# Scaling softmax weights: one VectorE multiplication with repeated inverse sums in place of two VectorE and two ScalarE operations

## The chip, the cores and the metric

The kernel runs on one core of a Trainium2 chip. The metric is the device time of one execution in microseconds (us); the median of the runs is used. The core's engines are named as in the profile: PE (TensorE, matmuls and transposes), DVE (VectorE), ACT (ScalarE), POOL (GpSimd) and SP (SyncE). POOL and SP mostly issue DMAs here. Each engine works through its own queue in order and waits at its head for semaphores of the others.

## What is computed

One layer of a streaming encoder: 1024 tokens, width 1024, float32. The part that the change touches is the attention with a window of three 64-token chunks, 16 query heads and 2 key/value heads of 64 dimensions, and a learned sink for each head:

```python
s = einsum('bnqhgd,bnkhd->bhgnqk', qc, kb) * HEAD_DIM ** -0.5
s = where(valid, s, -1e30)
m = maximum(max(s, axis=-1), sink)
p = exp(s - m)
denom = sum(p, axis=-1) + exp(sink - m)
o = einsum('bhgnqk,bnkhd->bnqhgd', p / denom, vb)
```

Before it stands one RMSNorm and a large input projection (queries, keys, values, gates and the inputs of the second branch); after it the gates, two output projections, the residual and a last RMSNorm. The change concerns `p / denom`.

## The kernel before, in words

**The matmul frame.** Most of the time goes into projections. They are done two output tiles at a time by `gemm_pair` (a "pair"), as seven products of 512 x 512 quarters with pre-added operands, named by their right-hand forms `b11`, `t1`, `t2`, `b21`, `t3`, `b22`, `t4`, in this order. Each product is 12 matmuls of 128x512 (line L362): operands are split in a rounded high part and a low remainder, and high x high, high x low and low x high are added up. The weight halves `wh` (a cast on ACT, L176) and `wl` (a subtraction on DVE, L177) are made by `split_next` while products run; there are three buffers of each, so a cast waits until the product that read the buffer's old content is through. After some products ACT copies and DVE adds the accumulator (L380, L384, L387, L392, L397, L401).

**Attention rides in the hooks.** From about 305 us to 585 us the eleven pairs that project gates call a hook after each product, and the hook advances a generator, `attention()`. It goes through 32 steps: 2 key/value groups x 8 query tiles of 128 tokens x 2 parities. Counting from 0, step n is a `softmax_stage` in two halves (chunk c = 0, 1, each 64 queries of 4 heads laid out as two sets of 128 rows, i = 0, 1), the `weight_stage` of step n - 2 (transposes of the weights) and the `value_stage` of step n - 3 (weights times values). About three steps fall in one pair.

**One softmax step.** For each chunk PE makes two score tiles `ps_sc` (L1442), ACT copies them to `sl` (L1448), DVE adds their two halves, negates and takes the row bound into `nmax` (L1454, a custom instruction with a second one that reads its accumulator), and ACT exponentiates in place and sums the rows into `sums` (L1470, again with a read of the accumulator). The chunk's exponentials are issued behind the copies of the next chunk. After the second chunk `rest_of_step` adds the sink's share (L1484 on DVE, L1485 on ACT, L1486 on DVE), takes reciprocals `inv` (L1488) and scales the weights: chunk 0 by two `tensor_scalar_mul` on DVE (L1493), chunk 1 by two multiplications on ACT (L1495). The weights of a step lie in one tile `pr` of 128 x 2 x 384; chunk 1 has the first 192 columns and chunk 0 the last 192 (in the first query tile of a group, 128 and 64).

**What reads them.** In `weight_stage` PE transposes six blocks of `pr` (L1515, four in the first tile): first the two blocks that lie in chunk 0's columns, then the two in chunk 1's, then the two in the middle that hold both. ACT and DVE then split the transposed weights (`pT`, `pTb`), and PE multiplies them by the values (L1550, L1555). ACT copies and DVE adds the result into `aT` (L1563, L1564).

**Order.** The order of each engine's queue is made by the framework's scheduler from the program, its dependencies and `after` (an order without a wait). A change of one instruction can therefore move others.

Of the kernel before, what the change touches and what calls it, by code (L numbers as in the profile page):

```python
# [26 lines left out]
AF = mybir.ActivationFunctionType  # L27
# [3 lines left out]
P = 128  # L31
# [21 lines left out]
def hybrid_tile(  # L53
# [16 lines left out]
    nc = tc.nc  # L70
# [12 lines left out]
    def bank(tag, dt=F32):  # L83
        return psum.tile([P, 512], dt, name=nm("ps_" + tag), tag="ps_" + tag, bufs=2)

    def mtile(shape, dt, tag, bufs, pool=None):
        return (pool or main).tile(shape, dt, name=nm(tag), tag=tag, bufs=bufs)
# [11 lines left out]
    def after(second, first):  # L99

        tc.add_manual_dep(
            second.ins,
            first.ins.name,
            mybir.DependencyInfo(mybir.DependencyClass.NoSync, mybir.DependencyReason.DATA),
            reason="order",
        )
# [521 lines left out]
    def scale_of(t):  # L628
        xt = x_in[t] if t in x_in else load_x(t)
        ss = mtile([P, 1], F32, "st1", 16)  # L630
        if t < 1:
            base = mtile([P, 1], F32, "st1", 16)
            square = nc.scalar.activation(junk[:, 0:HALF], xt[:, 0:HALF], AF.Square, accum_out=ss[:])
            z = xt[:, HALF:D]
            by_vector = nc.vector.tensor_tensor_reduce(
                junk[:, HALF:D], z, z, 4.0 / D, 4.0 * EPS, op0=ALU.mult, op1=ALU.add, accum_out=base[:]
            )
            after(by_vector, g_low)
            squares.append(square)
            return xt, rstd_of(ss[:], 1.0 / D, base[:])  # L640
        square = nc.scalar.activation(junk[:], xt[:], AF.Square, accum_out=ss[:])
        squares.append(square)
        if t == 7:
            after(square, casts[11])
        elif t > 2:

            after(square, casts[2 * t - 3])
        return xt, rstd_of(ss[:], 1.0 / D)
# [197 lines left out]
    first = scale_of(0)  # L846
# [259 lines left out]
    bias = []  # L1106
# [310 lines left out]
    def small():  # L1417
        return mtile([P, 2, 2], F32, "sm", 12, aheads)

    def window_of(t, c):  # L1420

        return (64 * c, 64 * c + 192) if t else (P, P + 64 * (c + 1))

    def softmax_stage(g, t, par, qt):

        kt = keys[g, t][0]
        q_of = qt[:].rearrange("p i (q c) -> p c (i q)", c=2)
        nmax, sums = small(), small()  # L1430
        n_pr[0] += 1
        pr = mtile([P, 2, 384], F32, f"pr{n_pr[0] % 2}", 1, weights_pool)
        held_in = {}
        sinks_of = (v[:, 4 * g + par : 4 * g + par + 3 : 2] for v in (sink_sb, nsink_sb))
        sk, nsk = sinks_of
        for c in range(2):
            lo, hi = window_of(t, c)
            wide = hi - lo
            scores, halves, copies = [], [], []
            for i in range(2):  # L1440
                sc = bank("sc")[:, 0 : 2 * wide].rearrange("p (f k) -> p f k", f=2)
                nc.tensor.matmul(  # L1442
                    sc, q_of[:, c, i * P : (i + 1) * P], kt[:, :, lo:hi], start=True, stop=True
                )
                scores.append(sc)
            for i, sc in enumerate(scores):
                two = mtile([P, 2, 192], F32, "sl", 2, aheads)[:, :, 0:wide]
                copies.append(nc.scalar.copy(two, sc))  # L1448
                halves.append(two)
            for i, two in enumerate(halves):  # L1450
                at = 192 * (1 - c) if t else P * (1 - c)
                held_in[c, i] = v = pr[:, i, at : at + wide]
                bounds.append(
                    nc.vector.tensor_tensor_reduce(  # L1454
                        v,
                        two[:, 0, :],
                        two[:, 1, :],
                        1.0,
                        nsk[:, i : i + 1],
                        op0=ALU.add,  # L1460
                        op1=ALU.min,
                        accum_out=nmax[:, c, i : i + 1],
                    )
                )
            finish_chunk(copies[-1])

            def rest_of_chunk(copied, c=c):
                for i in range(2):
                    v = held_in[c, i]
                    e = nc.scalar.activation(  # L1470
                        v, v, AF.Exp, bias=nmax[:, c, i : i + 1], scale=-1.0, accum_out=sums[:, c, i : i + 1]
                    )
                    if copied is not None:
                        after(e, copied)
                if c == 1:
                    rest_of_step()

            unfinished.append(rest_of_chunk)
            if c == 0:
                yield  # L1480

        def rest_of_step():
            es = small()
            nc.vector.tensor_add(es[:], sk.unsqueeze(1).broadcast_to([P, 2, 2]), nmax[:])  # L1484
            nc.scalar.activation(es[:], es[:], AF.Exp)  # L1485
            nc.vector.tensor_add(es[:], es[:], sums[:])  # L1486
            inv = small()
            nc.vector.reciprocal(inv[:], es[:])  # L1488
            for c in range(2):
                for i in range(2):  # L1490
                    v = held_in[c, i]
                    if c == 0:
                        nc.vector.tensor_scalar_mul(v, v, inv[:, c, i : i + 1])  # L1493
                    else:
                        nc.scalar.mul(v, v, inv[:, c, i : i + 1])  # L1495
            held.append(pr)

        yield
# [3 lines left out]
    def finish_chunk(copied=None):  # L1502

        if unfinished:
            unfinished.pop(0)(copied)
# [66 lines left out]
    def attention():  # L1572
# [14 lines left out]
        for n, step in enumerate(steps):  # L1587
            if n >= 2:
                weigh(n - 2)
                yield  # L1590
            halves = softmax_stage(*step, qT.pop(0))
            next(halves)
            yield
            next(halves)
            if n + 2 < len(steps):
                qT.append(query_stage(*steps[n + 2]))
            if n in (0, 2):
                value_loads(*tiles[n // 2])
            yield
            if n >= 3:  # L1600
                value(n - 3)
                yield
# [427 lines left out]
    for p in range(4):  # L2030
        n, t, acc, x11 = N_PAIRS + p, T_ORDER[p], accs[p], firsts[p]
# [92 lines left out]
        wide = HALF // 2  # L2124
# [98 lines left out]
```

## Time and profile before

| | |
|---|---|
| median of 3 runs | 894.31 us (894.05 to 894.41) |
| profiled execution | 894.7 us, its span 892.9 us |
| granted PE clock, mean | 0.998 |
| busy over the span | PE 99%, PE weight loads 82%, DVE 77%, ACT 65%, POOL 17% |
| chain that ended last | PE 92%, ACT 3%, DVE 2% |

The span is the time from the first to the last instruction of the program; the execution's own time is 1.8 us longer. A busy PE is not one at its peak: matmuls overlap their successors, and a record of 0.39 us can be followed by the next after 0.23 us. To see what PE loses at a place, compare start times, not busy shares. In listings by time, the columns are the start, the duration, the engine, the line, the operation, what it writes and reads, and how many instructions were merged; in square brackets the idle time before it and what ended it.

### The profile page before, as it was taken

The numbers are of one execution on the slowest core, as the hardware profiler recorded it, in microseconds if no ns is written. First come the engines' busy times: TensorE is split into PE (matmuls) and PEld (weight loads), VectorE is DVE, ScalarE is ACT, GpSimd is POOL, SyncE is SP. The second block draws the span as 40 slices with busy tenths as digits, with TensorE's granted clock in tenths as the row PEclk, the third lists the DMA queues.
The fourth block names the chain that finished last, engine by engine and source line by source line (L and its number), as shares of the span: only waits on it lengthen the run. The fifth ranks groups of instructions, "written<-read, shape, count | busy, mean of one in ns | idle before, by whom it ended". The sixth has DMA issues, their size and how long they took to land.

```text
span 892.9 us, 13164 instructions
## 1 busy us (share of the span) xinstructions
PE 881.7 (99%) x4117; PEld 731.4 (82%) x4117; DVE 684.9 (77%) x1362; ACT 580.1 (65%) x1189; POOL 150.9 (17%) x217
## 2 busy tenths in 40 slices
PE   8999999999999999999999999999999999999996
PEld 6888888888888888888888888888888888888885
DVE  7979966566686778888878888847796578579886
ACT  6875533334445489989989899955685385467443
POOL 3322222203030001111211011101121121110012
PEclk9999999999999999999999999999999999999999
DMA  9998888958778667888786789989899789998533
GB/s 332 211 268 222 268 206 172 176 153 265 250 252 286 214 189 189 210 185 195 179 236 210 237 225 222 250 290 383 308 289 376 276 231 258 298 307 282 179 119 118
DMA packets 131410, 212.40 MB, mean 238 GB/s; under 512 B 12778, under 2 KB 59882, under 8 KB 131340
## 3 DMA queue, kind: packets, MB, share of 16 engines
q1 hardware_dynamic: 108808, 148.62, 50.0%
q0 software_dynamic: 22384, 62.67, 31.6%
q8 instruction: 33, 0.54, 0.2%
q14 instruction: 37, 0.30, 0.1%
q10 hardware_dynamic: 148, 0.27, 0.1%
HBM read 146.37 MB, written 86.11 MB: 260 GB/s over the span
## 4 chain that ended last, share of the span: by engine, by line
PE 92%; ACT 3%; DVE 2%; issue 1%; DMA 1%; POOL 0%; SPq 0%; ACTq 0%; DVEq 0%
PE ps_mm L362 42%; PE ps_o L362 24%; PE ps_tp L362 7%; PE ps_sc L362 3%; PE ps_tp L793 2%; PE ps_o L793 2%; PE ps_mm L793 2%; PE ps_tp L1515 2%; PE ps_sc L1442 2%; PE ps_tp L1112 2%; PE ps_o L1550 1%; PE ps_sc L793 1%; ACT wh L176 1%; DVE wl L177 1%; PE ps_o L1555 1%
## 5 line engine op out<-in xcount | busy, mean ns | idle before, releaser
L176 ACT CAST wh<-s 128x1024 fp32r<-128x1024 f32 (+1 forms) x79 | 79.4, 1006 | 75.2 <-PE ps_mm L362 23.5
L177 DVE TENSOR_TENSOR wl<-wr,wh 128x512 fp32r<-128x512 f32 (+1 forms) x77 | 72.0, 937 | 58.0 <-ACT wh L176 57.9
L177 DVE TENSOR_TENSOR wl<-s,wh 128x1024 fp32r<-128x1024 f32 (+1 forms) x79 | 92.9, 1176 | 11.8 <-ACT wh L176 11.7
L176 ACT CAST wh<-wr 128x512 fp32r<-128x512 f32 (+1 forms) x77 | 63.0, 819 | 55.9 <-PE ps_mm L362 31.5
L1448 ACT COPY sl<-ps_sc 128x384 f32<-128x384 f32 (+2 forms) x128 | 51.8, 456 | 9.9 <-DVE sm L1454 9.9
L362 PE MATMUL ps_o<-T_t1h,wh 128*128 128x512 f32 x148 | 57.9, 391 | 0.0
L362 PE MATMUL ps_o<-T_t1h,wl 128*128 128x512 f32 x148 | 57.7, 390 | 0.0
L362 PE MATMUL ps_o<-T_t1l,wh 128*128 128x512 f32 x148 | 57.6, 389 | 0.0
L1470 ACT ACTIVATE pr<-pr,sm 128x192 f32<-128x192 f32 (+2 forms) x128 | 56.2, 444 | 0.1
L1454 DVE CUSTOM_DVE_ANT_0 pr<-sl,nsink_sb 128x192 f32<-128x192 f32 (+2 forms) x128 | 48.0, 399 | 9.9 <-ACT sl L1448 8.8
L362 PE MATMUL ps_mm<-T_b11h,wh 128*128 128x512 f32 x140 | 54.9, 392 | 0.0
L362 PE MATMUL ps_mm<-T_t3h,wh 128*128 128x512 f32 x140 | 54.7, 390 | 0.0
L362 PE MATMUL ps_mm<-T_b11l,wh 128*128 128x512 f32 x140 | 54.6, 390 | 0.0
L362 PE MATMUL ps_mm<-T_t2h,wh 128*128 128x512 f32 x140 | 54.6, 390 | 0.0
L362 PE MATMUL ps_mm<-T_b11h,wl 128*128 128x512 f32 x140 | 54.6, 390 | 0.0
L362 PE MATMUL ps_mm<-T_t3h,wl 128*128 128x512 f32 x140 | 54.6, 390 | 0.0
L362 PE MATMUL ps_mm<-T_t2l,wh 128*128 128x512 f32 x140 | 54.6, 390 | 0.0
L362 PE MATMUL ps_mm<-T_t3l,wh 128*128 128x512 f32 x140 | 54.5, 390 | 0.0
L362 PE MATMUL ps_mm<-T_t2h,wl 128*128 128x512 f32 x140 | 54.5, 389 | 0.0
L362 PE MATMUL ps_mm<-T_t4h,wh 128*128 128x512 f32 x136 | 53.2, 391 | 0.3 <-DVE x L397 0.3
L362 PE MATMUL ps_mm<-T_t4h,wl 128*128 128x512 f32 x136 | 53.0, 390 | 0.0
L362 PE MATMUL ps_mm<-T_t4l,wh 128*128 128x512 f32 x136 | 52.9, 389 | 0.0
(432 smaller groups left out, 2448.5 us busy)
## 6 DMA issues: line engine op xcount, KB each, us to landing
wr<-in_w_dram SPq DMA_DIRECT2D x86, 256.0 KB
sums<-in_w_dram POOLq DMA_DIRECT2D x20, 512.0 KB, 7.0
s<-sums SPq DMA_DIRECT2D x20, 512.0 KB
q_hl<-qhl SPq DMA_DIRECT2D x16, 512.0 KB
q<-q_hl SPq DMA_DIRECT2D x64, 128.0 KB
y_dr<-x POOLq DMA_DIRECT2D x28, 256.0 KB, 6.8
g<-in_w_dram POOLq DMA_DIRECT2D x12, 512.0 KB, 6.8
wr<-in_w_dram SPq DMA_DIRECT2D x11, 512.0 KB
```

The source lines that it names most:

```text
L176: hi_of.append(nc.scalar.copy(hi, src))
L177: lo_of.append(nc.vector.tensor_sub(lo, src, hi.bitcast(F32)))
L362: nc.tensor.matmul(acc, lt, rt, start=fresh and k == 0 and n == 0, stop=k == 3 and n == 2, skip_group_check=True,)
L793: mm = nc.tensor.matmul(acc[:], lt, rt, start=fresh and k == 0 and n == 0, stop=stops and k == 3 and n == terms[-1], skip_group_check=True,)
L1112: nc.tensor.matmul(pm[:, t * P : (t + 1) * P], xh[:, half * 4 + t, g * P : (g + 1) * P], bias[-1][1][:, g % 4, :], start=True, stop=True,)
L1442: nc.tensor.matmul(sc, q_of[:, c, i * P : (i + 1) * P], kt[:, :, lo:hi], start=True, stop=True)
L1448: copies.append(nc.scalar.copy(two, sc))
L1454: nc.vector.tensor_tensor_reduce(v, two[:, 0, :], two[:, 1, :], 1.0, nsk[:, i : i + 1], op0=ALU.add, op1=ALU.min, accum_out=nmax[:, c, i : ...
L1470: e = nc.scalar.activation(v, v, AF.Exp, bias=nmax[:, c, i : i + 1], scale=-1.0, accum_out=sums[:, c, i : i + 1])
L1515: nc.tensor.transpose(dst, pr[:, i, block * P : block * P + width], ident[:])
L1550: nc.tensor.matmul(po[:, first], va[1][:, vs], a[:, n, first], start=n == 0, stop=n == 1, skip_group_check=True)
L1555: nc.tensor.matmul(po[:, cs], vb[c][:, vs], b[c][:], start=t == 0, stop=True, skip_group_check=True)
```

## The change

The four scalings of a step become one `tensor_mul` on DVE over the whole tile `pr`, whose second operand is `inv` read with a step of zero along the columns (two such instructions in each of the four steps on a group's first tile, since the two chunks have different widths there). For that, `nmax`, `sums` and so `inv` are stored by place in `pr`: chunk c at index 1 - c.

```diff
-                        accum_out=nmax[:, c, i : i + 1],
+                        accum_out=nmax[:, 1 - c, i : i + 1],
...
-                        v, v, AF.Exp, bias=nmax[:, c, i : i + 1], scale=-1.0, accum_out=sums[:, c, i : i + 1]
+                        v, v, AF.Exp, bias=nmax[:, 1 - c, i : i + 1], scale=-1.0, accum_out=sums[:, 1 - c, i : i + 1]
...
-            for c in range(2):
-                for i in range(2):
-                    v = held_in[c, i]
-                    if c == 0:
-                        nc.vector.tensor_scalar_mul(v, v, inv[:, c, i : i + 1])
-                    else:
-                        nc.scalar.mul(v, v, inv[:, c, i : i + 1])
+            spans = ((0, 2, 384),) if t else ((0, 1, P), (1, 1, 64))
+            start = 0
+            for first, chunks, wide in spans:
+                v = pr[:, :, start : start + wide].rearrange("p i (c k) -> p i c k", c=chunks)
+                by = inv[:, first : first + chunks].rearrange("p c i -> p i c").unsqueeze(3)
+                nc.vector.tensor_mul(v, v, by.broadcast_to(list(v.shape)))
+                start += wide
```

The scheduler then orders some neighbours in another way. The first place is PE's queue behind the product `t3` of a pair, where the transposes of a step stand (step 12; the other pairs with such a place read alike). Before:

```order
L362 MATMUL ps_mm_4054<-T_t3h_754,wl_4034 128x512
L1515 MATMUL ps_tp_4278<-ident,pr_761_4090 128x128 x4
L1515 MATMUL ps_tp_4286<-ident,pr_761_4090 128x128 x2
L1442 MATMUL ps_sc_4298<-k_4140,q_4142 128x384
L1442 MATMUL ps_sc_4300<-k_4140,q_4142 128x384
L362 MATMUL ps_o_4113<-T_b22h_398,wh_4033 128x512
```

And now:

```order
L1442 MATMUL ps_sc_4261<-k_4106,q_4108 128x384
L1515 MATMUL ps_tp_4241<-ident,pr_761_4059 128x128 x4
L1515 MATMUL ps_tp_4249<-ident,pr_761_4059 128x128 x2
L1442 MATMUL ps_sc_4263<-k_4106,q_4108 128x384
L362 MATMUL ps_o_4079<-T_b22h_398,wh_4002 128x512
```

One of the two score matmuls now stands ahead of the transposes (at step 3 both do, and the first matmul of `b22` as well). The second place is ACT's queue half a pair earlier, from the copy behind `t1` (L384) to the cast of the weights of `t4` (L176), where the ACT scalings of step 11 stood. Before:

```order
L384 ACTIVATE x_4057<-ps_o_4113 128x512
L1495 ACTIVATE pr_727_3962<-pr_727_3962,sm_4107 128x192 x2
L1448 COPY sl_4132<-ps_sc_4128 128x384
L1448 COPY sl_4134<-ps_sc_4130 128x384
L1470 ACTIVATE pr_761_4090,sm_4089<-pr_761_4090,sm_4088 128x192 x2
L1563 COPY aT_4046<-ps_o_4145 64x2x4x64
L176 CAST wh_4171<-wr_3698 128x512
```

And now:

```order
L384 ACTIVATE x_4026<-ps_o_4079 128x512
L1448 COPY sl_4098<-ps_sc_4094 128x384
L1448 COPY sl_4100<-ps_sc_4096 128x384
L1470 ACTIVATE pr_761_4059,sm_4058<-pr_761_4059,sm_4057 128x192 x2
L1563 COPY aT_4015<-ps_o_4111 64x2x4x64
L176 CAST wh_4137<-wr_3676 128x512
```

Nothing else moved there; the two scalings are gone and all behind them stands directly behind L384. The third place is DVE's queue at the seam of the two groups (steps 15 and 16), between the row bounds of step 16 and the update L397 of an accumulator that PE's product `t4` waits for. It reads L262, L1564, L263, L264, L265, L397 before; now it reads L1564, L262, L264, L263, L397, L265, so that L397 stands behind four operations instead of five. On SP some loads changed places with neighbours (weights `wr`, keys `k`, values `vb`, stores of `x`); POOL's order is the same.

## The prediction

> **What bounds the kernel now.** I read the page first, then the busy times by stage, then what PE waits for in the attention stage, then the chain and the queues around its longest waits.
>
> ```profile
> 305.00:585.00 280.00, 277.90 (x1362) 232.06 (x1361) 230.18 (x660) 249.16 (x694) 39.15 (x50) 1.00 0.79 210
> ```
>
> The columns after the length are PE, weight loads, DVE, ACT and POOL. In the only stage that the change touches PE is busy for 277.9 of 280 us. ACT (249.2) is fuller than DVE (230.2); over the whole kernel it is the other way round. So nothing can be won but what PE loses here by waiting:
>
> ```profile
> PE ps_tp L1515 <- DVE pr L1493: 1.7, 6, 0.3
> PE ps_mm L362 <- DVE x L397: 0.3, 1, 0.3
> PEld ps_tp L1515 <- PE ps_mm L362: 5.0, 8, 0.7
> PEld ps_sc L1442 <- ACT sl L1448: 1.2, 6, 0.3
> ```
>
> The transposes of the weights (L1515) wait for exactly the scaling that is changed. The third row has eight waits, all in front of transposes (the release is put down to PE, which had long been done); they are the eight steps 3, 6, 9, 12, 21, 24, 27 and 30, whose transposes stand behind `t3`. In all other steps they stand behind `t2` or `b11`, and the listing by time has them 0.8 to 2.9 us behind the end of the scaling, the marginal step 1 apart. One of the eight, step 12:
>
> ```profile
> 417.11 0.39 PE L362 MATMUL ps_mm<-T_t3h,wl 128*128 128x512 f32 x1
> 417.20 0.80 ACT L1495 ACTIVATE pr<-pr,sm 128x192 f32<-128x192 f32 x2
> 417.34 0.54 DVE L1493 TENSOR_SCALAR pr<-pr,sm 128x192 f32<-128x192 f32 x2
> 417.80 0.90 PE L1515 MATMUL ps_tp<-ident,pr 128*128 128x128 f32 x6 [0.31 <-DVE pr L1493]
> 418.46 0.60 PE L1442 MATMUL ps_sc<-k,q 128*128 128x384 f32 x2
> 418.90 0.39 PE L362 MATMUL ps_o<-T_b22h,wh 128*128 128x512 f32 x1
> ```
>
> Matmuls of 128x512 follow each other by 0.23 us, so PE could have begun at 417.34 and began at 417.80: 0.46 us lost. What decides is therefore when the scaling starts and how long it takes. The chain tells where its start comes from (start, length, what):
>
> ```profile
> 409.82 0.57 ACT aT L1563
> ...
> 414.41 0.95 ACT wh L176
> ...
> 415.38 1.22 DVE wl L177
> ...
> 417.42 0.25 DVE pr L1493
> ...
> 417.80 0.79 PE ps_tp L1515 x5
> ```
>
> It is ACT's queue, from 409.8 to 415.4 without a pause, and then the subtraction `wl` on DVE that waits for ACT's last cast and stands ahead of the reciprocal and the scaling. ACT's queue further back:
>
> ```profile
> 406.76 0.58 ACT L384 ACTIVATE x<-ps_o 128x512 f32<-128x512 f32 x1
> 407.36 0.80 ACT L1495 ACTIVATE pr<-pr,sm 128x192 f32<-128x192 f32 x2
> 408.07 0.84 ACT L1448 COPY sl<-ps_sc 128x384 f32<-128x384 f32 x2
> 409.18 0.39 PE L362 MATMUL ps_mm<-T_t2l,wh 128*128 128x512 f32 x1
> 409.25 0.45 ACT L1470 ACTIVATE pr<-pr,sm 128x192 f32<-128x192 f32 x1
> 409.81 0.58 ACT L1563 COPY aT<-ps_o 64x512 f32<-64x512 f32 x1
> 410.42 0.62 ACT L176 CAST wh<-wr 128x512 fp32r<-128x512 f32 x1
> ```
>
> ACT is late here by its own work: the scores that L1448 copies and the sums that L1563 copies had been made 1.9 and 2.8 us before. Among that work are the two scalings of step 11, which the change removes. How far ACT can move ahead is limited by the cast at 410.42, which must wait until the `t2` product has read the buffer: its last matmul with `wh` starts at 409.18 and ends at 409.57.
>
> **The change part by part.** The durations (busy us, mean ns):
>
> ```profile
> L1493 DVE TENSOR_SCALAR pr<-pr,sm 128x192 f32<-128x192 f32 x56 | 15.3, 315 | 0.4
> L1495 ACT ACTIVATE pr<-pr,sm 128x192 f32<-128x192 f32 x56 | 22.4, 447 | 3.2 <-DVE sm L1488 3.0
> L262 DVE TENSOR_TENSOR s<-wr 128x512 f32<-128x512 f32 x23 | 15.8, 686 | 6.8 <-DMA wr<-in_w_dram 4.9 <-issue 1.8
> L177 DVE TENSOR_TENSOR wl<-s,wh 128x1024 fp32r<-128x1024 f32 x71 | 87.5, 1232 | 11.8 <-ACT wh L176 11.7
> ```
>
> *The new instruction.* No row has 128x768 with a repeated operand. Bounds are the 512 (0.686 us) and the 1024 (1.232 us) of the same operation; halfway between lies 0.96 us, and I take that, since a zero step asks for no more data. Against 0.54 us for the two it replaces, the scaling ends 0.42 us later from the same start, and DVE does 28 x 0.42 = 12 us more in the stage (230 to 242 of 280).
>
> The Trainium skill, "VectorE: DVE Perf Modes" (section "The perf-mode tier table"), speaks against the change: float32 `tensor_tensor` runs at one element a cycle, `tensor_scalar` at two. Its formula, (N + 151) / 0.96, gives an estimate of 957 ns for 768, which is what the two rows above give, so the sum by it is the same. What the rule leaves out is ACT's part.
>
> *ACT's relief.* 56 operations of 0.447 us go (22.4 us busy), and 8 more in the first tiles. On the path lies only the pair that stands ahead of the cast at 410.42: without it L1448 starts 0.8 us sooner, and so does all behind it down to the cast, which can go back from 410.42 to 409.60 at most. From there on chain and order are as before, so the scaling of step 12 would start at about 417.34 - 0.80 = 416.54. By the listing steps 21, 24 and 30 are like it (their casts start 0.8 to 0.9 us after the buffer is free). In the others the cast already stands near that limit:
>
> ```profile
> 332.10 0.39 PE L362 MATMUL ps_mm<-T_t2l,wh 128*128 128x512 f32 x1
> 332.71 0.62 ACT L176 CAST wh<-wr 128x512 fp32r<-128x512 f32 x1
> 339.76 0.54 DVE L1493 TENSOR_SCALAR pr<-pr,sm 128x192 f32<-128x192 f32 x2
> 341.56 0.39 PE L362 MATMUL ps_o<-T_b22l,wh 128*128 128x512 f32 x1
> 383.38 0.39 PE L362 MATMUL ps_mm<-T_t2l,wh 128*128 128x512 f32 x1
> 384.16 0.62 ACT L176 CAST wh<-wr 128x512 fp32r<-128x512 f32 x1
> 391.21 0.54 DVE L1493 TENSOR_SCALAR pr<-pr,sm 128x192 f32<-128x192 f32 x2
> 392.78 0.39 PE L362 MATMUL ps_o<-T_b22h,wh 128*128 128x512 f32 x1
> ```
>
> Step 3 can win 0.19 us (332.52 against 332.71) and step 9 0.36 (383.80 against 384.16); steps 6 and 27 are like 9.
>
> *PE's new order.* At seven places one score matmul stands ahead of the transposes and fills the wait; behind them stays one of two (0.44 / 2 = 0.22 us, 418.46 to 418.90). At step 3 both and the first of `b22` go ahead. The transposes take 0.66 us where the last ones wait for ACT (417.80 to 418.46) and 0.57 us where nothing holds them, which is now everywhere:
>
> ```profile
> 409.64 0.82 PE L1515 MATMUL ps_tp<-ident,pr 128*128 128x128 f32 x6
> 410.21 0.60 PE L1442 MATMUL ps_sc<-k,q 128*128 128x384 f32 x2
> 446.69 0.69 DVE L397 TENSOR_TENSOR x<-x,ps_mm 128x512 f32<-128x512 f32 x1
> 447.43 0.50 PE L362 MATMUL ps_mm<-T_t4h,wh 128*128 128x512 f32 x1 [0.27 <-DVE x L397]
> ```
>
> From the last two rows PE starts 0.05 us after DVE ends (447.38 to 447.43).
>
> *The sum by place*, as the new start of `b22`: scaling start + 0.96 + 0.05 + 0.57 + 0.22.
> - Step 12: 416.54 + 1.80 = 418.34 against 418.90, -0.56. PE itself is there with its score matmul at 417.34 + 0.22 = 417.56, just when the scaling is done, so hardly more can come. With 21, 24, 30: 4 x -0.5 = -2.0 (step 30, the last, has no scores; taken alike).
> - Step 9: 390.85 + 1.80 = 392.65 against 392.78; with 6 and 27: 3 x -0.1 = -0.3.
> - Step 3: 339.57 + 0.96 + 0.05 + 0.57 = 341.15 and a little for the second matmul of `b22` against 341.56: -0.35.
> - L397 at the seam has one addition fewer ahead (-0.69) and 0.42 more of scaling: -0.25, nearly the whole of the 0.27 us in the row.
> - Elsewhere: step 1's scalings move ahead of a `wl` that is needed much later; the transposes that stand behind `t2` and `b11` keep 0.4 us at the least; the moved loads on SP were early by the waits above, which name no load. Nothing.
>
> Together -2.9 us: from the profiled execution's 894.7 to 891.8, and, since the median stands 0.39 lower, to **891.4**.
>
> At the lower bound of the multiplication (0.686) only the steps that wait longest for DVE gain more: 3 x -0.23 and -0.25, so 890.5. At the upper (1.232): 8 x 0.27 = +2.2, so 893.6.
>
> **The rivals.**
> *The relief does not arrive.* ACT reaches the cast earlier, but something else holds the chain: a load, the copy of `t2`'s accumulator, DVE's own work ahead of `wl`. For it speaks that step 3 is already at the limit; against it, that the casts of four steps are far from it. Then each of the seven places goes from 417.34 + 1.56 to + 1.80, +0.24, step 3 gains 0.17, the seam 0.25: +1.3, 895.6. Half a relief gives about 893.4.
>
> *VectorE becomes what the chain waits for* (slower). Place: the pieces of DVE between the scaling of one step and the `wl` ahead of the next late one. DVE has 0.42 us more to do there; if no idle time takes it up, the scaling starts 0.42 us later without any relief, and a place costs 0.24 + 0.42 = 0.66: 8 x 0.66 - 0.6 = +4.7, 899.0. It decides where DVE's slack there is below 0.42 us. At step 11 it is well above:
>
> ```profile
> 410.42 0.69 DVE L1564 TENSOR_TENSOR aT<-aT,ps_o 64x512 f32<-64x512 f32 x1 [1.06 <-ACT aT L1563]
> ```
>
> That idle time waits for ACT, though, and shrinks as ACT gets faster.
>
> The Trainium skill's rate rule (the page above) would, if VectorE alone counted, mean this case.
>
> *The price is lost and won in equal parts*, PE's own pace showing as now: 894.3.
>
> **How the numbers follow.** About 0.2% (1.8 us) is what a measurement of this kernel can tell from no change, that is 892.5 to 896.1. The forecast with its relief whole or nearly so (890.4 to 892.5) has 0.55, all of it faster. Half a relief, none, or an even trade (893 to 895.8): 0.34, the same. VectorE as the bound, with all that costs more than I see: 0.11, slower. The range that leaves no more than 2 in 10 outside runs from 890.3 (the lower bound of the multiplication) to 895.7 (no relief); the likeliest case alone from 890.4 to 892.5.
>
> **What the next profile shows.** Right: one instruction of 128x768 at 0.93 to 0.99 us; ACT's busy time in the stage down by 22 to 26 us and DVE's up by about 12; the cast before the late places starting within 0.1 us of the buffer's release in all pairs; the eight waits before L1515 shorter in sum; the wait for L397 below 0.1 us; the stages before 305 us and after 585 us unchanged. Wrong: a multiplication above 1.2 us; the cast no earlier against the `t2` product than now; or new waits of PE on `wl`, `pT` or `x`, which would say that DVE's 12 us have come onto the path.

## The result, and the profile after

The changed kernel takes 892.28 us (median; 891.59 to 894.72), the kernel before 894.14 in the same comparison (893.65 to 895.0): a ratio of 0.9978 (95% interval 0.9970 to 0.9986), 1.9 us less. The forecast was 891.4 us, 2.9 less.

The profiled execution of the change has a span of 889.8 us, 3.1 less than that of before. Not all of that is the change. The starts of PE's products tell where it lies: the first row of each kernel below is the first pair after the start-up, the second the pair with which attention begins, the third the first product after attention. Before, then after:

```profile
94.26 0.39 PE L362 MATMUL ps_mm<-T_b11h,wh 128*128 128x512 f32 x1
...
301.50 0.39 PE L362 MATMUL ps_mm<-T_b11h,wh 128*128 128x512 f32 x1
...
581.21 0.40 PE L362 MATMUL ps_mm<-T_b11h,wh 128*128 128x512 f32 x1
```

```profile
93.04 0.39 PE L362 MATMUL ps_mm<-T_b11h,wh 128*128 128x512 f32 x1
...
300.27 0.39 PE L362 MATMUL ps_mm<-T_b11h,wh 128*128 128x512 f32 x1
...
578.05 0.40 PE L362 MATMUL ps_mm<-T_b11h,wh 128*128 128x512 f32 x1
```

The start-up, whose code is the same, was 1.22 us shorter in this one execution; in the twelve traces of this study it ends anywhere from 92.97 to 94.80 us. From there to the stage are 207.23 us in both, and behind the stage 311.71 (892.92 - 581.21) and 311.75. The stage itself went from 279.71 to 277.78: **-1.93 us**, close to the timed difference of 1.9. Below, "the stage" always means this difference of two product starts, which the start-up doesn't touch. It comes from one trace of each kernel.

Busy time in the window that the prediction showed (same columns):

```profile
305.00:585.00 280.00, 278.29 (x1371) 233.74 (x1370) 240.26 (x630) 227.31 (x627) 39.18 (x50) 1.00 0.79 211
```

ACT has 21.9 us less, DVE 10.1 more, and DVE is now the fuller of the two. The new instruction, then PE's waits of the stage (PE are its matmuls and transposes, PEld the loads of their weights; the rows for L397 and for the scores are gone):

```profile
L1494 DVE TENSOR_TENSOR pr<-pr,sm 128x768 f32<-128x768 f32 x28 | 26.7, 955 | 0.4
```

```profile
PEld ps_tp L1515 <- PE ps_sc L1442: 3.5, 7, 0.6
PE ps_tp L1515 <- DVE pr L1494: 1.2, 4, 0.5
PEld ps_tp L1515 <- issue: 0.9, 1, 0.9
PEld ps_tp L1515 <- PE ps_mm L362: 0.5, 1, 0.5
```

The rows of PE and of PEld show the same places from two sides, so they are not added. Call the eight steps of the prediction the late places. There PE's weight loads waited 5.0 us before and wait 4.0 now (3.5 + 0.5); the row of 0.9 is a ninth place, step 31. So the late places are still late, although the work in front of them comes earlier. Step 12 again:

```profile
415.21 0.96 DVE L1494 TENSOR_TENSOR pr<-pr,sm 128x768 f32<-128x768 f32 x1
415.65 0.39 PE L362 MATMUL ps_mm<-T_t3h,wl 128*128 128x512 f32 x1
415.88 0.34 PE L1442 MATMUL ps_sc<-k,q 128*128 128x384 f32 x1
416.31 0.85 PE L1515 MATMUL ps_tp<-ident,pr 128*128 128x128 f32 x6
416.92 0.43 PE L1442 MATMUL ps_sc<-k,q 128*128 128x384 f32 x1
417.18 0.39 PE L362 MATMUL ps_o<-T_b22h,wh 128*128 128x512 f32 x1
```

Measured from the last matmul of `t3` (417.11 before, 415.65 now), the scaling starts 0.67 us earlier (+0.23 before, -0.44 now), and `b22` 0.26 us earlier (1.79, now 1.53). The rest is lost between the start of the longer instruction and `b22`. The cast that opens the chain now waits for its buffer, which the last matmul of `t2` with it releases at 408.24:

```profile
407.85 0.39 PE L362 MATMUL ps_mm<-T_t2l,wh 128*128 128x512 f32 x1
408.28 0.62 ACT L176 CAST wh<-wr 128x512 fp32r<-128x512 f32 x1 [0.74 <-PE ps_mm L362]
```

### The profile page after: what moved, and what is told of

Same layout as the page of the kernel before. It is cut to its first block, busy times and chain, and to the rows that moved or that the text cites. A ratio compares the mean times of both kernels' runs of the same rounds, so it can differ in the third digit from the quotient of the medians.

```text
span 889.8 us, 13051 instructions
## 1 busy us (share of the span) xinstructions
PE 879.4 (99%) x4117; PEld 732.1 (82%) x4117; DVE 695.6 (78%) x1334; ACT 558.6 (63%) x1125; POOL 151.7 (17%) x217
## 4 chain that ended last, share of the span: by engine, by line
PE 93%; DVE 2%; ACT 2%; DMA 1%; issue 1%; POOL 0%; SPq 0%; ACTq 0%
PE ps_mm L362 43%; PE ps_o L362 24%; PE ps_tp L362 7%; PE ps_sc L362 3%; PE ps_tp L793 2%; PE ps_o L793 2%; PE ps_tp L1515 2%; PE ps_mm L793 2%; PE ps_sc L1442 2%; PE ps_tp L1112 2%; PE ps_o L1550 1%; PE ps_sc L793 1%; PE ps_o L1555 1%; PE ps_sc L663 1%; DVE wl L177 1%
## 5 line engine op out<-in xcount | busy, mean ns | idle before, releaser
L176 ACT CAST wh<-s 128x1024 fp32r<-128x1024 f32 (+1 forms) x79 | 79.4, 1007 | 77.9 <-PE ps_o L362 21.9
L176 ACT CAST wh<-wr 128x512 fp32r<-128x512 f32 (+1 forms) x77 | 63.1, 821 | 62.7 <-PE ps_mm L362 38.2
L1448 ACT COPY sl<-ps_sc 128x384 f32<-128x384 f32 (+2 forms) x128 | 52.7, 459 | 13.6 <-DVE sm L1454 10.1
```

The lines of the kernel that those rows point to most:

```text
L176: hi_of.append(nc.scalar.copy(hi, src))
```

## Experiments

Every kernel was timed against the kernel before. Line numbers are each kernel's own, so the transposes (L1515) stand between L1511 and L1520 in some. "Stage" is the difference of the two product starts against that of before, from one trace each. The interval of a ratio is about 0.9 us either way, so e2 and e5 can't be told from the kernel before by their times, nor e4, e6 and e9 from the change. Outside the stage the twelve traces agree within 0.1 us, but for e8 (0.3 us more ahead of the stage and 0.4 behind it) and e9 (0.2 more behind it).

| kernel | median us | ratio (95%) | stage us |
|---|---|---|---|
| the change | 892.28 | 0.9978 (0.9970 to 0.9986) | -1.93 |
| e1 ACT pair left out, DVE pair kept | 888.62 | 0.9943 (0.9930 to 0.9955) | -5.16 |
| e2 change + ACT pair back on spare data | 894.34 | 1.0004 (0.9995 to 1.0013) | +0.59 |
| e3 four short scalings on DVE | 890.47 | 0.9959 (0.9946 to 0.9971) | -3.31 |
| e4 change, scaling ahead of the row bounds | 892.61 | 0.9982 (0.9973 to 0.9991) | -1.21 |
| e5 change, PE's old order | 893.60 | 0.9993 (0.9984 to 1.0002) | -0.27 |
| e6 multiplication in two halves | 891.91 | 0.9975 (0.9966 to 0.9985) | -1.83 |
| e7 e3 + one score matmul first | 890.30 | 0.9960 (0.9947 to 0.9974) | -4.14 |
| e8 change + 0.84 us more DVE work a step | 896.53 | 1.0028 (1.0017 to 1.0039) | +2.02 |
| e9 four short tensor_mul | 892.39 | 0.9981 (0.9972 to 0.9990) | -1.93 |
| e10 chunk 1 on GpSimd | 895.81 | 1.0016 (1.0007 to 1.0025) | +1.36 |

### e1: the relief alone

```diff
-            for c in range(2):
-                for i in range(2):
-                    v = held_in[c, i]
-                    if c == 0:
-                        nc.vector.tensor_scalar_mul(v, v, inv[:, c, i : i + 1])
-                    else:
-                        nc.scalar.mul(v, v, inv[:, c, i : i + 1])
+            for i in range(2):
+                v = held_in[0, i]
+                nc.vector.tensor_scalar_mul(v, v, inv[:, 0, i : i + 1])
```

> The kernel before, with the two ACT scalings left out (the 192 columns of chunk 1 stay unscaled, so that part of the result is not computed) and the two on DVE kept; PE's order is that of the kernel before. It has ACT's relief without the longer multiplication and without the new PE order. Theory A (the gain of the change is ACT's relief, the longer multiplication takes part of it back): the scaling starts at all late places 0.2 to 0.7 us earlier against the product t3, as in the changed kernel, and as the first transposes need only the first 0.315 us of scaling, PE hardly waits: about -3 us at the late places and -1 us at the seam and before the scores, 890.1 us. Theory B (the gain comes from the score matmul that now stands ahead of the transposes, and the relief moves nothing): no gain, 894.1. Theory C (start-up of the program differs, not the attention stage): 894.1, and the stage as long as before.

Measured: 888.62 us, stage -5.16. The scaling starts as early as in the changed kernel, and the transposes wait only at step 3, by 0.26 us (the group of all transposes in the stage; the last figure is PE's idle time before them):

```profile
L1511 PE MATMUL ps_tp<-ident,pr 128*128 128x128 f32 (+1 forms) x184 | 25.3, 272 | 0.1
```

So ACT's relief is worth about 5 us to this stage, more than I had expected, and the change keeps two of them. The kernel leaves the 192 columns of chunk 1 unscaled, so its transposes wait for no scaling of their own: the 5 us are the relief with nothing paid for chunk 1. B and C fall.

### e2: the pair back on ACT

```diff
+    spare = weights_pool.tile([P, 192], F32, name="spare")
...
+            for i in range(2):
+                w = spare[:, 0 : (192 if t else 64)]
+                nc.scalar.mul(w, w, inv[:, 0, i : i + 1])
             held.append(pr)
```

> The changed kernel with two ACT multiplications of 128x192 put back in each step, on a spare tile that nobody reads, behind the same reciprocal. It has the new multiplication and PE's new order, without ACT's relief. Theory A: the scaling starts at the late places as late as in the kernel before, and PE's next product starts 1.97 us after the start of the scaling instead of 1.56: +0.41 us at seven places, about +2.7 against the kernel before, 896.8 us. Theory B (PE's new order makes the gain): 892.3, as the changed kernel. The forecast's rival 'the relief does not arrive', with the lag from DVE to PE at 0.05, said 895.6.

Measured: 894.34 us, stage +0.59: without the relief the gain is gone, though PE's order is that of the change (but for step 31, whose transposes stand behind the first matmul of `t4`). B falls a second time. A's size was wrong (+2.7 expected). One reason is in ACT's row:

```profile
L1500 ACT ACTIVATE spare<-spare,sm 128x192 f32<-128x192 f32 x56 | 25.1, 449 | 0.4 <-DVE sm L1490 0.2
PE ps_tp L1520 <- DVE pr L1496: 3.5, 9, 0.6
```

The pair's work is back (25.1 us; 22.4 before), its waiting is not: before, ACT stood idle 3.2 us ahead of L1495, for the reciprocal; here 0.4, since the scheduler put the spare pair a little later. At step 12 the scaling starts 2.40 us after the start of `t3`, between 2.77 before and 2.08 in the change. The experiment took back most of the relief, not all.

### e3: the same work in four pieces

```diff
-                    if c == 0:
-                        nc.vector.tensor_scalar_mul(v, v, inv[:, c, i : i + 1])
-                    else:
-                        nc.scalar.mul(v, v, inv[:, c, i : i + 1])
+                    nc.vector.tensor_scalar_mul(v, v, inv[:, c, i : i + 1])
```

> The kernel before with all four scalings on DVE as four tensor_scalar of 128x192 (4 x 0.315 us = 1.26 us instead of one of 0.955); ACT has the same relief; PE's order at the late places is that of the kernel before. Theory A: the first transposes are ready 0.46 us after the start of the scaling and the last at about 1.40 us, and the next product starts about 2.17 us after the start of the scaling, 0.2 us later than with the one multiplication: about 8 x 0.2 more than the changed kernel, 893.9 us. Theory D (ACT's relief alone counts, DVE's longer work lies beside PE's): 890 to 892.3.

Measured: 890.47 us, stage -3.31, better than the change by 1.4. My sum of 4 x 0.315 = 1.26 was wrong. Step 12, the four merged in one row:

```profile
414.96 1.00 DVE L1492 TENSOR_SCALAR pr<-pr,sm 128x192 f32<-128x192 f32 x4
415.36 0.40 PE L362 MATMUL ps_mm<-T_t3h,wl 128*128 128x512 f32 x1
415.60 0.97 PE L1512 MATMUL ps_tp<-ident,pr 128*128 128x128 f32 x6
416.32 0.61 PE L1442 MATMUL ps_sc<-k,q 128*128 128x384 f32 x2
416.78 0.39 PE L362 MATMUL ps_o<-T_b22h,wh 128*128 128x512 f32 x1
```

Four follow each other in 0.23 us and are done in 1.00, against 0.96 for the one. But PE begins to transpose right behind `t3` (415.36 + 0.24), while DVE is still scaling chunk 1, and `b22` starts 1.42 us after the last matmul of `t3` instead of 1.53. DVE is as full as in the change:

```profile
305.00:585.00 280.00, 279.92 (x1376) 235.58 (x1375) 241.84 (x722) 226.51 (x628) 39.14 (x50) 1.00 0.79 212
```

### e4: the scaling ahead of the row bounds

```diff
+            finish_chunk(copies[-1])
             for i, two in enumerate(halves):
                 ...
-            finish_chunk(copies[-1])
```

> The changed kernel with finish_chunk called ahead of the row bounds of the next chunk and not behind them, so that on DVE the reciprocal and the multiplication stand ahead of two custom instructions (0.34 us each) with their two reads. Theory A (at the late places the start of the scaling decides, and it stands behind work that nobody needs yet): it starts 0.6 us earlier, the transposes wait no more, 8 x -0.3 us: about 889.9. Theory E: the row bounds come a microsecond later, and with them the next exponentials on ACT, which then makes the casts and copies late: 892.3 to 894.

Measured: 892.61 us, stage -1.21. The scaling comes two microseconds earlier against `t3` than in the change (step 12: 0.23 us after its start, 2.08 there), and the transposes and `b22` no longer wait (PE's order came out as that of the kernel before). But what this wins is lost again before and behind `t4`:

```profile
PEld ps_mm L362 <- DVE x L397: 2.9, 7, 0.6
```

```profile
420.49 0.68 DVE L397 TENSOR_TENSOR x<-x,ps_mm 128x512 f32<-128x512 f32 x1
421.22 0.50 PE L362 MATMUL ps_mm<-T_t4h,wh 128*128 128x512 f32 x1
```

The row bounds, which stood ahead of the scaling, now stand behind it and ahead of the accumulator update L397. At step 12 L397 starts 6.25 us after the start of `t3`, where it starts 5.35 in the change, and PE waits for it seven times. It is the forecast's kind of new wait, on another instruction than theory E named. Up to the last pair this only uses up the gain; the 0.7 us by which the stage is longer than in the change come mostly (0.55) from the last pair. There PE's value matmuls wait 0.73 us:

```profile
570.58 0.67 DVE L1564 TENSOR_TENSOR aT<-aT,ps_o 64x512 f32<-64x512 f32 x1
571.40 0.70 PE L1550 MATMUL ps_o<-pT,v 128*128 128x512 f32 x2 [0.73 <-ACT pr L1470]
```

The profile names ACT's exponentials, which make nothing that these matmuls read. In ten of the twelve traces they start 0.06 to 0.16 us behind the end of L1564, the addition that reads the values before them (here 571.25 and 571.40). In e4 the row bounds of step 31 come late ahead of that addition: it starts 3.95 us after the start of `t3`, where it starts 2.99 in the change. So it is DVE's new order that costs here too.

### e5: PE's old order

`turns` holds the last transpose that was issued; first the matmuls of the products, then the scores of chunk 0:

```diff
+                if turns:
+                    after(mm, turns[0])
...
+                if c == 0 and turns:
+                    after(score, turns[0])
...
+            turns[:] = [nc.tensor.transpose(dst, pr[:, i, block * P : block * P + width], ident[:])]
```

> The changed kernel, with orders (no waits) that put PE's queue back to that of the kernel before: the two score matmuls and the next product stand behind the transposes. ACT's relief and the one multiplication stay. Theory A (the forecast's term of 0.22 us for one score matmul ahead of the transposes): the transposes start when the multiplication is done, as in the changed kernel, and both score matmuls follow: +0.22 us at seven places, and about 0.3 at step 3, so 894.1 us, and the gain of the change is gone. Theory F (PE's order matters little, because what runs ahead of the transposes is only late elsewhere): 892.3 to 892.8.

Measured: 893.60 us, stage -0.27. PE's order is worth 1.66 us of the change's 1.93 (1.3 by the medians), close to A's 1.8. F falls. The weight loads ahead of the eight late transposes wait longer than in the kernel before (5.0):

```profile
PEld ps_tp L1520 <- PE ps_mm L363: 6.3, 8, 1.1
```

e1 has the same PE order and the same relief: the one multiplication of all columns instead of two short scalings of chunk 0 costs -0.27 + 5.16 = 4.9 us there. So without PE's new order the relief and the price of the long multiplication nearly cancel.

### e6: the multiplication in two halves

```diff
+            for c in range(2):
+                at = 192 * (1 - c) if t else P * (1 - c)
+                wide = 192 if t else 64 * (c + 1)
+                v = pr[:, :, at : at + wide]
+                by = inv[:, 1 - c, :].unsqueeze(2)
+                nc.vector.tensor_mul(v, v, by.broadcast_to(list(v.shape)))
```

> The changed kernel with the one tensor_mul of 128x768 split into two of 128x384, chunk 0's columns first, so that the operation is the same and only its length differs; PE's order at the late places comes out as that of the kernel before. Theory G (what costs is that nothing of a long instruction can be read before its end; four short ones follow each other in 0.23 us and the transposes run behind them): the first transposes are ready after about 0.55 + 0.14 us, the others after about 1.0 + 0.14; the next product starts 3.9 to 4.1 us after the start of t3, as with the four short ones, so 890.5 to 891. Theory H (it is tensor_tensor against tensor_scalar that matters): 892.3 or more.

Measured: 891.91 us, stage -1.83; by the median between G's 890.5 to 891 and H's 892.3.

```profile
415.70 1.02 DVE L1494 TENSOR_TENSOR pr<-pr,sm 128x384 f32<-128x384 f32 x2
```

The stage is 1.56 us shorter than in e5, but not all of that is the cut: at step 3 the scheduler put a score matmul ahead of the transposes, and at step 30 the first matmul of `b22` ahead of the values. At the late places 6, 9, 12, 21, 24 and 27, where PE's order is that of e5, `b22` starts 0.12 to 0.16 us earlier against `t3` than there, 0.86 in sum. So waiting for the end of one long instruction does cost. Four short ones (e3) bring 2.0 us at the same six places; with two halves, all of chunk 1 is ready only at the end of the second.

### e9: four short tensor_mul

```diff
-                    if c == 0:
-                        nc.vector.tensor_scalar_mul(v, v, inv[:, c, i : i + 1])
-                    else:
-                        nc.scalar.mul(v, v, inv[:, c, i : i + 1])
+                    nc.vector.tensor_mul(v, v, inv[:, c, i : i + 1].broadcast_to(list(v.shape)))
```

> The four scalings on DVE as in e3, but each as a tensor_mul of 128x192 with the inverse sum repeated, in place of a tensor_scalar; PE's order at the late places is that of e3. From the rows of 128x128 (0.284 us) and 128x256 (0.423 us) one takes about 0.354 us, and with the overlap of neighbours that the four tensor_scalar show (0.085 us) they follow each other in 0.27: the last ends 1.16 us after the first starts, against 1.00 in e3 and 1.03 with two halves. Theory G (short pieces let the transposes run behind them; the kind of operation only sets the pitch): the last transposes come 0.16 us later than in e3 at seven places, the stage -2.2 us against the kernel before, about 891.7 us. Theory H (the kind decides, however it is cut): the stage as with the two halves or worse, -1.8 or less, 892 us and more.

Measured: 892.39 us, stage -1.93: hardly better than two halves, between G's -2.2 and H's -1.8, and the interval of the time holds both.

```profile
415.71 1.16 DVE L1492 TENSOR_TENSOR pr<-pr,sm 128x192 f32<-128x192 f32 x4
```

They follow each other in 0.27 us as expected and fill DVE for 4.8 us more than e3 in the window; the last piece ends later by 0.16 us. At the six late places 6 to 27, where PE's order is that of e3 and e5, `b22` comes 0.15 us later than in e3 on the mean and 0.18 earlier than with the one long multiplication of e5. That is G's reading: cutting helps with either operation, and the operation sets how much. But four pieces of this kind gain little over two halves (0.14 earlier than e5).

### e7: one score matmul first

The first score matmul of a step is made ahead of the transposes of step n - 2, with an order between them:

```diff
+            turn = nc.tensor.transpose(...)
+            if ahead_mm is not None:
+                after(turn, ahead_mm)
```

> The four short scalings on DVE, with one score matmul ordered ahead of the transposes, as the changed kernel has it at seven places. Theory G: with the four short scalings the next product starts 3.87 to 4.06 us after t3, against 3.77 where nothing is waited for; the score matmul fills 0.22 us of that, and all of it goes: about 8 x -0.17, 889.1 us. Theory F: no gain, 890.5. It could become slower where the score matmul itself has to wait for its bank.

Measured: 890.30 us, stage -4.14, 0.83 better than e3 by the stage, where G said 1.4; the two medians (890.47 and 890.30) can't tell that. At the six late places 6 to 27 `b22` now starts 3.76 to 3.82 us after `t3`, where e3 has 3.87 to 4.06: hardly anything is left to wait for. This and e3 are the versions with the whole result that beat both kernels; their intervals just touch that of the change.

### e8: more work on DVE

```diff
+    spare = weights_pool.tile([P, 256], F32, name="spare")
...
+            for i in range(2):
+                by = inv[:, 0, i : i + 1].broadcast_to([P, 256])
+                nc.vector.tensor_mul(spare[:], spare[:], by)
             held.append(pr)
```

> The changed kernel with two spare tensor_mul of 128x256 on DVE in each step behind the multiplication, on a tile that nobody reads: about 0.8 us more of DVE work in a step, 26 us in the stage, twice what the change added. Theory A (DVE has room; only work that stands ahead of the late scalings counts): 892.3 to 893.3 us. The forecast's rival (VectorE becomes what the chain waits for): 0.8 us at each of the eight late places and at the seam, 898 to 899.

Measured: 896.53 us, stage +2.02 (its last values run into the next product, so 0.4 us more falls behind the stage), 3.95 more than the change, between the theories:

```profile
305.00:585.00 280.00, 277.26 (x1351) 228.87 (x1351) 261.29 (x696) 228.04 (x628) 39.15 (x50) 1.00 0.77 207
PEld ps_tp L1520 <- PE ps_mm L362: 7.9, 17, 0.8
```

With DVE at 261 of 280 us, 17 transposes wait in this row alone, where eight waited before: steps that had time to spare have none. By the product starts PE loses 0.3 to 0.6 us more than in the change between `t2` and `b21` in eight of the pairs, and 0.1 to 0.3 less between `t3` and `b22` in six. So the sign of the rival comes true, but not its place: the eight late places don't pay, others do. "DVE has room" is true only up to a point. How much of that the first 10 us cost, which the change adds, stays open: e3 costs 1.85 us against e1, and that holds both DVE's load and the later readiness of chunk 1.

### e10: chunk 1 on GpSimd

```diff
+                    engine = nc.gpsimd if c else nc.vector
+                    engine.tensor_scalar_mul(v, v, inv[:, c, i : i + 1])
```

> The kernel before with the two scalings of chunk 1 on GpSimd in place of ACT; DVE keeps its two of chunk 0; PE's order at the late places is that of the kernel before. It computes all, with ACT's whole relief and DVE's short scalings, so the limit is the run without the ACT pair (stage -5.16 us, about 888.6 to 889.5 us). No row shows an arithmetic instruction of GpSimd. Up to 0.4 us each: chunk 1 is ready when PE comes to it, 889. At 1 us each: the transposes of chunk 1 wait until about 4.2 us after t3 instead of 2.97, 1.2 us at each of eight places against a gain of 5: about 899. A GpSimd that slows DVE's own instructions down would add to that.

Measured: 895.81 us, stage +1.36:

```profile
L1493 DVE TENSOR_SCALAR pr<-pr,sm 128x192 f32<-128x192 f32 x56 | 22.0, 434 | 0.4
L1493 POOL TENSOR_SCALAR pr<-pr,sm 128x192 f32<-128x192 f32 x56 | 44.0, 798 | 117.4 <-DVE sm L1488 89.0 <-ACT x L384 28.4
PEld ps_tp L1513 <- POOL pr L1493: 4.4, 10, 0.6
```

GpSimd takes 0.80 us for one, PE waits for it, and DVE's own scalings beside it take 434 ns instead of 315.

## Why the prediction was right, and where its sizes were not

The direction and the mechanism hold: ACT's relief moves the late places ahead, and the long multiplication takes part of it back. e1 and e2 show the relief (-5.16 without the price, +0.59 without most of the relief), e5 that the change needs PE's new order too (-0.27 without it). That the total came within 1.0 us of the forecast is in part luck: terms that were too good by 2.2 us and terms that were missing or too small by 1.2 us stand against each other. Term by term, from the product starts:

- *Late places 12, 21, 24 and 30: forecast 4 x -0.5.* Measured -0.29, -0.18, -0.22 and -0.41, together -1.1. The casts start 0.04 us behind the release of their buffers in all eleven pairs, as forecast, and the scaling 0.58 to 0.69 us earlier against the start of `t3` (0.80 forecast). The term that was mis-sized is "scaling start + 0.96 + 0.05 + 0.57 + 0.22": it is 1.97 us at step 12 (415.21 to 417.18), not 1.80. The lag from DVE to PE is 0.14 (416.17 to 416.31), transposes 0.61, score 0.26. The 0.05 was read from L397 and the product behind it. The right row was in the quoted listing: the first transpose before started at 417.80, 0.14 after the end of the *first* short scaling (417.34 + 0.32). I had read it as waiting for both, so I charged 0.42 us where the first transpose became ready 0.64 later.
- *Steps 9, 6 and 27: forecast 3 x -0.1.* Measured about +0.2 together: the scaling starts 0.30 to 0.41 us earlier, as forecast (0.36), and the same mis-sized term uses that up.
- *Step 3: forecast -0.35.* Measured -0.17.
- *One score matmul ahead "at seven places".* It is six: 6, 9, 12, 21, 24 and 27. At step 30, which has no scores, the first matmul of `b22` goes ahead instead (568.22, the transposes at 568.70).
- *L397 at the seam: forecast -0.25.* Measured -0.52, the wait and what it had made late. The forecast took PE's row (0.27); the weight load in front of the same product had waited longer, in a row that the prediction did not use:

```profile
PEld ps_mm L362 <- DVE x L397: 0.5, 1, 0.5
```

  L397 ends now at 445.16, 0.11 ahead of `t4`:

```profile
444.47 0.69 DVE L397 TENSOR_TENSOR x<-x,ps_mm 128x512 f32<-128x512 f32 x1
445.27 0.43 PE L362 MATMUL ps_mm<-T_t4h,wh 128*128 128x512 f32 x1
```

- *"Elsewhere ... Nothing" was wrong twice.* The row "PEld ps_sc L1442 <- ACT sl L1448: 1.2, 6" stood in the prediction and had no term. It is gone, and the products behind those score matmuls start 0.9 us earlier in sum. And step 31 became a late place. The prediction had all steps but the eight behind `t2` or `b11`; but the transposes of steps 0, 15 and 18 stand behind `t3` too, in time before and after, and those of step 31 behind `b22`, where they had 1.7 us to spare. Before, then after:

```profile
574.15 0.55 DVE L1493 TENSOR_SCALAR pr<-pr,sm 128x192 f32<-128x192 f32 x2
...
576.17 0.39 PE L362 MATMUL ps_o<-T_b22h,wl 128*128 128x512 f32 x1
576.40 0.84 PE L1515 MATMUL ps_tp<-ident,pr 128*128 128x128 f32 x6
```

```profile
572.11 0.96 DVE L1494 TENSOR_TENSOR pr<-pr,sm 128x768 f32<-128x768 f32 x1
572.37 0.39 PE L362 MATMUL ps_o<-T_b22h,wl 128*128 128x512 f32 x1
573.22 0.85 PE L1515 MATMUL ps_tp<-ident,pr 128*128 128x128 f32 x6 [0.46 <-DVE pr L1494]
```

PE could have gone on at 572.60 (572.37 + 0.23) and went on at 573.22: +0.62. On DVE the scaling of this step had moved behind the splits of `pT` and `pTb`, which the order of the instructions could have told.

The sum of these is -1.9: against the forecast the late places brought 0.9 us less, the middle steps 0.5 less, step 3 0.2 less, and step 31 cost 0.6 (2.2 in all); the scores and the seam brought 1.2 more.

Of the rivals, "the relief does not arrive" is what e2 makes: its stage (+0.59) has the sign of the rival's +1.3 us, its time (1.0004, 0.9995 to 1.0013) can't tell it from no change. "Lost and won in equal parts" is close to e5, without PE's new order. "VectorE becomes the bound" is the direction of e8. Of the signs named beforehand: the multiplication at 955 ns and the cast within 0.1 us of its buffer came true, ACT's busy time fell by 21.9, just short of the 22 named; "the eight waits before L1515 shorter in sum" came true, 4.0 us against 5.0 by the weight loads, but a ninth wait came up; the wait for L397 is gone; and the stages before and behind stayed as they were but for the start-up.

## What to carry to other kernels

Taking work off a late engine is worth what its readers gain, and an instruction that makes one long result of four short ones hands it over all at once. At six places with the same order of PE, 0.96 us in one piece (e5) let the next product start 2.0 us later in sum than 1.00 us in four (e3), and 1.1 us later than four of its own kind that take 1.16 us (e9). When you price a wait, ask which piece of the producer the first reader needs, and take the lag from a row in which a reader waits for just that piece. Give every wait row that you quote a term in the sum.

## What the runs showed of the hardware

The two kinds of multiplication on DVE differ in slope and in fixed cost. From e9 (first three rows) and e3:

```profile
L1492 DVE TENSOR_TENSOR pr<-pr,sm 128x192 f32<-128x192 f32 x112 | 32.5, 352 | 0.4
L1492 DVE TENSOR_TENSOR pr<-pr,sm 128x128 f32<-128x128 f32 x8 | 1.9, 283 | 0.0
L1492 DVE TENSOR_TENSOR pr<-pr,sm 128x64 f32<-128x64 f32 x8 | 1.4, 221 | 0.1
```

```profile
L1492 DVE TENSOR_SCALAR pr<-pr,sm 128x192 f32<-128x192 f32 x112 | 28.2, 316 | 0.4
L1492 DVE TENSOR_SCALAR pr<-pr,sm 128x128 f32<-128x128 f32 x8 | 1.9, 282 | 0.0
L1492 DVE TENSOR_SCALAR pr<-pr,sm 128x64 f32<-128x64 f32 x8 | 1.7, 253 | 0.1
```

From 64 to 192 columns `tensor_tensor` grows by 1.02 ns an element ((352 - 221) / 128), `tensor_scalar` by 0.49. That is the factor of two of the Trainium skill, "VectorE: DVE Perf Modes" (section "The perf-mode tier table"), which the trace bears out. But the faster one starts from a higher fixed cost, so at 128 columns they are equal (283 and 282 ns), and at 64 `tensor_tensor` is the shorter (221 and 253). A repeated operand (step of zero) cost nothing that shows: 955 ns at 768 columns, where halfway between the plain rows of 512 and 1024 lies 959.

DVE's `tensor_scalar` went from 315 to 434 ns on the mean while GpSimd scaled beside it (e10). At step 12 two of them lie wholly beside GpSimd's and take 0.85 us, where two took 0.54 alone:

```profile
416.44 1.52 POOL L1493 TENSOR_SCALAR pr<-pr,sm 128x192 f32<-128x192 f32 x2 [2.90 <-DVE sm L1488]
416.47 0.85 DVE L1493 TENSOR_SCALAR pr<-pr,sm 128x192 f32<-128x192 f32 x2
```

The Trainium skill, "SBUF — State Buffer" (section "Who interferes with whom"), calls the port pair that both share an exclusive lock. That the two hinder each other agrees. But GpSimd started first, and its two instructions take until 417.96; DVE is through with both of its own at 417.32. A DVE that waited out even the first of them (half of 1.52 us) and then needed its 0.54 would have ended at about 417.74, so in these rows the hindrance is partial.
